# Two encoder layers on one core: the second MLP product by seven block products instead of eight

## The chip, the cores and the metric

The kernel runs on one core of one Trainium2 chip. The metric is the device time of one execution in microseconds (us). TensorE (PE in the profile) multiplies matrices into PSUM, VectorE (DVE), ScalarE (ACT) and GpSimd (POOL) do the elementwise work, and the queue of SyncE (SP) issues most of the loads from HBM.

## What is computed

The program is two layers of an encoder over 512 tokens of 1024 channels, in fp32. Each layer has four attention branches (A to D) that are gated, merged and projected, a LayerNorm, an MLP with a gated per-layer input, and a second LayerNorm. The lines that matter here are those of the MLP:

```python
h = layer_norm(alpha * h + merged @ w_out[i], ln1_g[i], ln1_b[i])
ff = jnp.square(jax.nn.relu(h @ w_ff1[i])) @ w_ff2[i]
ple = (p[i] @ w_ple[i]) * jax.nn.sigmoid(h @ w_ple_gate[i])
h = layer_norm(alpha * h + ff + ple, ln2_g[i], ln2_b[i])
```

`w_ff1` is 1024 by 4096 and `w_ff2` is 4096 by 1024.

## The kernel before

**Arithmetic.** PE reads operands of type fp32r. A factor x is held as two such tiles: hi, the rounded copy of x, and lo, which is x - hi. A product of two factors takes three matmuls, hi by hi, lo by hi and hi by lo (the list `SEQ3`). The tile `R` has 64 slots of 128x512 for hi and lo parts; 16 of them hold the residual stream h, and 48 are given out by an allocator (`P.ar`).

**Weights.** All weights come in chunks of 128x1024 (512 KB), in one list that `plan_layer` writes in the order of use. SP loads a chunk into one of two raw buffers; ACT copies it to its hi slots (line 106, called in `split_next`), and POOL subtracts to make its lo slots (line 170). `take` is called where PE's work on a chunk is written; it first writes out loads and splits up to some chunks ahead (`look`, `extra`), as far as slots are free.

**Order.** Nothing is scheduled: each engine runs its instructions in the order in which the program writes them, each waiting for what it needs. So an instruction that waits holds back everything behind it on its engine.

**MLP before.** Per layer there are 32 chunks of `w_ff1`. For each, PE makes 24 matmuls of 512 columns into one bank (`gemm_T`, line 94), ACT takes the relu out of PSUM (line 1291), DVE squares it (1293), ACT makes hi (106) and DVE makes lo (109). The 32 hidden tiles are taken in groups of 12, 12 and 8. After each group, `outer` multiplies them with the group's chunks of `w_ff2`: for either half f of the 1024 output columns, each chunk (two hidden tiles by 512 columns) takes 24 matmuls of 512 columns, six into each of four banks, one bank for 128 tokens. At the end of a half DVE adds the four banks to the residual rows `FD` (1303, 1305). The second product thus takes 32 chunks of 24 matmuls, 768 a layer.

**Branch B.** The last projection tile of stage A makes B's keys. `evac_k2` writes hi of either head into one half of the partitions of its slot and copies it into the other half by DVE (lines 365 and 366). The first score matmuls of branch B stand at the start of the next `run`, which deals out the steps of an attention branch evenly between the parts of the main work.

## Time and profile before

| | |
|---|---|
| time, median of 3 runs | 1996.1 us (1995.84 to 1997.12) |
| the profiled execution, its time | 1997.37 us |
| the profiled execution, its span | 1995.5 us |
| TensorE busy | 1954.3 us (98%), 9440 matmuls |
| VectorE busy | 777.1 us (39%) |
| ScalarE busy | 755.2 us (38%) |
| GpSimd busy | 840.3 us (42%) |
| granted TensorE clock, mean | 0.997 |

The span is the time from the first to the last instruction of the profiled execution; the 1.9 us beside it lie around the program. Busy time is that in which an engine works on at least one instruction. The profile says of each idle stretch of an engine which other instruction ended it; for one that isn't on the path that ends last, such idle time costs nothing.

### The profile page before, as it was taken

The page shows a single profiled execution, that of the slowest core. Times are in us where ns is not written, and L with a number is a line of the kernel's source. Part 1 is how long each engine was busy: PE and PEld are TensorE (multiplying, and loading weights), DVE is VectorE, ACT ScalarE, POOL GpSimd, SP SyncE. Part 2 cuts the span into 40 slices and gives each one's busy share as a digit, 9 for nine tenths or more (in the row PEclk, how much of TensorE's full clock was granted, in tenths as well). Part 3 has the DMA queues.
Part 4 walks back from the last instruction along what each step waited for, and adds up shares of the span by engine and source line. Part 5 has one row for each costly group of instructions (what it writes and reads, how often), then busy time and mean ns, then how long its engine had stood idle before and what let it go on. Part 6 is the DMA issues. An engine that isn't in the chain of part 4 may idle for free.

```text
span 1995.5 us, 24072 instructions
## 1 busy us (share of the span) xinstructions
PE 1954.3 (98%) x9440; PEld 1611.4 (81%) x9440; DVE 777.1 (39%) x1565; ACT 755.2 (38%) x1313; POOL 840.3 (42%) x407
## 2 busy tenths in 40 slices
...
GB/s 168 108 54 82 99 112 97 89 82 61 147 117 95 96 126 74 107 87 103 122 111 68 57 82 103 82 125 72 101 56 168 96 102 101 102 84 127 67 120 78
DMA packets 59697, 195.96 MB, mean 98 GB/s; under 512 B 6720, under 2 KB 11968, under 8 KB 59584
## 3 DMA queue, kind: packets, MB, share of 16 engines
...
## 4 chain that ended last, share of the span: by engine, by line
PE 66%; DVE 3%; ACT 1%; POOL 1%; DMA 1%; issue 1%; DVEq 0%; ACTq 0%; POOLq 0%
PE PS L94 64%; PE PS L97 2%; ACT R L106 1%; POOL R L170 1%; DVE R L109 1%; DMA raw<-in_wO_dram 0%; DMA raw<-in_wPL_dram 0%; DVE gate L1254 0%; DVE FD L303 0%; DVE FD L301 0%; DVE p L394 0%; ACT p L386 0%; DVE qf L916 0%; DVE ysum L421 0%; DVE rt L915 0%
## 5 line engine op out<-in xcount | busy, mean ns | idle before, releaser
L94 PE MATMUL PS<-R 128*128 128x512 f32 (+4 forms) x8528 | 1886.2, 378 | 12.3 <-DVE R L365 5.3
L94 PEld LDWEIGHTS PS<-R 128*128 128x128 f32 (+1 forms) x8528 | 1508.5, 187 | 333.0 <-issue 37.6
L170 POOL TENSOR_TENSOR R<-raw,R 128x1024 fp32r<-128x1024 f32 (+1 forms) x304 | 734.7, 2421 | 848.5 <-ACT R L106 811.2
L106 ACT ACTIVATE R<-raw 128x1024 fp32r<-128x1024 f32 x306 | 321.1, 1053 | 340.8 <-PE PS L94 143.5
L106 ACT ACTIVATE R<-PS 128x128 fp32r<-128x128 f32 (+5 forms) x300 | 131.7, 450 | 131.9 <-PE PS L97 82.3
L109 DVE TENSOR_TENSOR R<-PS,R 128x512 fp32r<-128x512 f32 (+5 forms) x276 | 134.4, 494 | 118.7 <-ACT R L106 117.5
L1109 POOL TENSOR_TENSOR M<-M,gate 128x512 f32<-128x512 f32 x48 | 62.1, 1293 | 191.7 <-DVE gate L1108 135.5
L386 ACT ACTIVATE p<-p,s 128x256 f32<-128x256 f32 (+2 forms) x96 | 66.1, 688 | 187.1 <-DVE s L551 65.4
L1293 DVE TENSOR_TENSOR ff<-relu 128x512 f32<-128x512 f32 x64 | 44.3, 692 | 222.1 <-ACT relu L1291 222.1
L1305 DVE TENSOR_TENSOR FD<-FD,PS 128x512 f32<-128x512 f32 x40 | 27.5, 687 | 242.5 <-PE PS L94 242.5
L1291 ACT ACTIVATE relu<-PS 128x512 f32<-128x512 f32 x64 | 38.3, 599 | 168.5 <-PE PS L94 168.5
L394 DVE TENSOR_SCALAR p<-p,s 128x512 f32<-128x512 f32 (+3 forms) x128 | 95.0, 742 | 4.5
L97 PE MATMUL PS<-ident,p 128*128 128x128 f32 x480 | 73.6, 273 | 2.8 <-DVE p L394 1.7
L97 PEld LDWEIGHTS PS<-ident,p 128*128 128x128 f32 x480 | 58.6, 140 | 16.1 <-DVE p L394 2.5
L109 DVE TENSOR_TENSOR R<-ff,R 128x512 fp32r<-128x512 f32 x64 | 44.3, 692 | 47.6 <-ACT R L106 47.6
L1108 DVE SCALAR_TENSOR_TENSOR gate<-gate,PS 128x512 f32<-128x512 f32 x48 | 32.9, 686 | 71.1 <-ACT gate L1104 42.8
L106 ACT ACTIVATE R<-ff 128x512 fp32r<-128x512 f32 x64 | 40.5, 632 | 50.9 <-DVE ff L1293 50.9
L393 DVE RECIPROCAL s<-s 128x1 f32<-128x1 f32 x128 | 20.9, 163 | 79.3 <-ACT p L386 78.1
L277 POOL TENSOR_TENSOR s<-s,mhalf 128x1 f32<-128x1 f32 x18 | 21.4, 1192 | 71.9 <-DVE s L275 71.9
L627 DVE CUSTOM_DVE_ANT_0 p<-PS,bd 128x512 f32<-128x512 f32 x32 | 21.8, 682 | 76.1 <-PE PS L94 76.1
L386 ACT ACTIVATE p<-PS,s 128x512 f32<-128x512 f32 x32 | 22.0, 689 | 53.2 <-DVE s L481 53.0
L106 ACT ACTIVATE R<-M 128x512 fp32r<-128x512 f32 (+3 forms) x20 | 13.8, 695 | 62.3 <-POOL M L1109 52.7
...
## 6 DMA issues: line engine op xcount, KB each, us to landing
raw<-in_wF_dram SPq DMA_DIRECT2D x128, 512.0 KB, 3.4
raw<-in_wT_dram SPq DMA_DIRECT2D x106, 512.0 KB, 3.5
raw<-in_wBR_dram SPq DMA_DIRECT2D x16, 512.0 KB, 3.5
raw<-in_wO_dram SPq DMA_DIRECT2D x16, 512.0 KB, 3.6
raw<-in_wPG_dram SPq DMA_DIRECT2D x16, 512.0 KB, 3.4
raw<-in_wVD_dram SPq DMA_DIRECT2D x12, 512.0 KB, 3.4
hsp<-FD SPq DMA_DIRECT2D x8, 512.0 KB, 6.1
FD<-hsp SPq DMA_DIRECT2D x8, 512.0 KB, 5.9
```

The lines of the kernel that those rows point to most:

```text
L94: self.nc.tensor.matmul(out, l, r, start=start, stop=stop, skip_group_check=True)
L97: self.nc.tensor.transpose(out, in_, self.ident)
L106: self.nc.scalar.activation(out=out, in_=in_, func=AF.Copy, scale=scale)
L109: self.nc.vector.tensor_tensor(out=out, in0=a, in1=hi.bitcast(F32), op=ALU.subtract)
L170: nc.gpsimd.tensor_tensor(out=lo, in0=raw, in1=hi.bitcast(F32), op=ALU.subtract)
L386: P.nc.scalar.activation(out=pt[:, 0:n], in_=src, func=AF.Exp, bias=nm, scale=1.0, accum_out=den)
L394: nc.vector.tensor_scalar(out=pt[:, 0:n], in0=pt[:, 0:n], scalar1=rd, scalar2=0.5, op0=ALU.mult, op1=ALU.mult)
L1108: nc.vector.scalar_tensor_tensor(out=t, in0=t, scalar=1.0, in1=pb, op0=ALU.add, op1=ALU.mult)
L1109: nc.gpsimd.tensor_tensor(out=P.M[:, j, :], in0=P.M[:, j, :], in1=t, op=ALU.add)
L1291: nc.scalar.activation(out=r, in_=ps, func=AF.Relu)
L1293: nc.vector.tensor_tensor(out=f, in0=r, in1=r, op=ALU.mult)
L1305: nc.vector.tensor_tensor(out=u, in0=u, in1=ps, op=ALU.add)
```

## The change

The second product of the MLP is made by Strassen's scheme in Winograd's form. Two hidden tiles (a pair) and 512 tokens make a left matrix of 2 by 2 blocks (hidden tile by half of the tokens), the two chunks of `w_ff2` that belong to the pair make a right one (hidden tile by half of the output columns). Seven products of blocks take the place of eight. The left factors are the blocks 11, 12 and 22 and four sums of blocks (`hidden`); the right factors are the blocks 11, 21 and 22 and four differences T1 to T4, which DVE makes in place in the raw buffers (`split_quad`). Each product takes 6 matmuls of 512 columns, three into each of two banks. There are 16 pairs a layer, in groups of 2, 3, 3, 3, 3 and 2; within a group each of the seven products runs over the group's pairs before the next begins. The first pair of the next group is made before a group's products.

Three pairs of banks (X, Y, Z) gather the products; X is read by DVE after P1, goes on with P6, is read again, and goes on with P7.

Raw buffers, the softmax tiles and some other tiles become parts of one tile `F`, so that in the MLP seven raw buffers can be had instead of two, and up to four chunks are loaded ahead. In `evac_k2` four ACT copies replace two ACT copies and two DVE copies; branch B's steps begin two parts later.

The tile `F` is what the orders below call the raw buffers, `ff` are squared hidden tiles, `fs` the sums of left blocks, `PS` PSUM, and `FD` the residual rows.

The core of the diff:

```diff
+U_P, U_PG, U_YS, U_RAW, N_UNIT = 16, 25, 29, 31, 39
...
-        self.raw_p = pool("raw", 2)
...
-        self.p_p = pool("pp", 3)
...
+        self.F = const.tile([128, N_UNIT, 256], F32, name="F")
+        self.M = self.F[:, 0:16, :].rearrange("p (a b) c -> p a (b c)", b=2)
+        self.pt = [self.units(U_P + 3 * i, 3) for i in range(3)]
+        self.pi = 0
+        self.ysum = self.units(U_YS, 2)
+        self.pg = self.units(U_PG, 4).rearrange("p (c t) -> p c t", c=4)
+        self.fa = Arena(N_UNIT)
+        self.fa.close(0, U_RAW)
...
-            self.load(self.cs + 2)
+            self.load(self.cs + self.depth)
...
+    def split_quad(self, c, only_make=False):
+
+
+        nc = self.nc
+        *q, what = c['quad']
+        (r0, u0), (r1, u1) = [self.raws.get(tuple(q) + (f,), (None, None)) for f in range(2)]
+        at = {'11': (r0, 0), '21': (r0, 512), '12': (r1, 0), '22': (r1, 512)}
+        b = lambda n: at[n][0][:, at[n][1]:at[n][1] + 512]
+        op = {'T1': ('11', '12', '11'), 'T2': ('11', '22', '11'), 'T3': ('12', '22', '12'), 'T4': ('21', '11', '21')}
+        src = what
+        if what in op:
+            src, x, y = op[what]
+            if not c.get('made'):
+                nc.vector.tensor_tensor(out=b(src), in0=b(x), in1=b(y), op=ALU.subtract)
+                c['made'] = True
+        if only_make:
+            return
+        c['k'] = 1
+        c['s'] = [self.ar.alloc(1) for _ in range(2)]
+        c['hi'], c['lo'] = [self.R[:, s, :] for s in c['s']]
+        self.acopy(c['hi'], b(src))
+        nc.gpsimd.tensor_tensor(out=c['lo'], in0=b(src), in1=c['hi'].bitcast(F32), op=ALU.subtract)
+        if what == 'T3':
+            self.fa.release(u1, 4)
+        elif what == 'T4':
+            self.fa.release(u0, 4)
...
+            self.split_quad(c)
+            self.cs += 1
+            if self.cs < self.cd and self.chunks[self.cs]['quad']:
+                self.split_quad(self.chunks[self.cs], True)
+            return
...
+    def run(self, main, other=(), after=0):
...
-                want = len(other) * seen // n_m
+                want = len(other) * max(seen - after, 0) // (n_m - after)
...
-    P.acopy(v(ka)[0:64], ps[0:64])
-    P.acopy(v(kb)[64:128], ps[64:128])
+    for x in (slice(0, 64), slice(64, 128)):
+        P.acopy(v(ka)[x], ps[0:64])
+        P.acopy(v(kb)[x], ps[64:128])
     P.vsub(v(kl)[0:64], ps[0:64], v(ka)[0:64])
     P.vsub(v(kl)[64:128], ps[64:128], v(kb)[64:128])
-    nc.vector.tensor_copy(ka[64:128], ka[0:64].bitcast(F32))
-    nc.vector.tensor_copy(kb[0:64], kb[64:128].bitcast(F32))
...
-FF_GROUPS = ((0, 12), (12, 24), (24, 32))
+
+FF_GROUPS = (2, 3, 3, 3, 3, 2)
+
+FF_LOOK = {'1': (2, 2, 9, 9), '2': (6, 1, 2, 0)}
+PRODUCTS = (('P1', '11'), ('P5', 'T1'), ('P6', 'T2'), ('P2', '21'), ('P3', '22'), ('P7', 'T3'), ('P4', 'T4'))
...
+def ff_order():
+
+    out, a = [], 0
+    for n in FF_GROUPS:
+        out += [('1', i) for i in range(a + bool(a), a + n)]
+        if a + n < 16:
+            out.append(('1', a + n))
+        out.append(('2', range(a, a + n)))
+        a += n
+    return out
...
+    for what, i in ff_order():
+        if what == '1':
+            for j in (2 * i, 2 * i + 1):
+                P.plan((l, 'f1', j), a['wF1'][l, j], 1024)
+            continue
+        for prod, right in PRODUCTS:
+            for q in i:
+                f = {'P1': 0, 'P5': 1}.get(prod)
+                P.plan((l, 'f2', prod, q), None if f is None else a['wF2'][l, f, q], 1024, quad=(l, q, right), half=f)
...
-    P.run(main, stB + pre(lambda: biasC(0)))
+    P.run(main, stB + pre(lambda: biasC(0)), 2)
...
-    for gi, (j0, j1) in enumerate(FF_GROUPS):
-        fs = []
-        for j in range(j0, j1):
-            w = P.take((l, 'f1', j))
-            ps = P.PS[:, P.bank(), :]
+
+    P.fa.close(0, 8, False)
+    P.fa.close(U_P, U_RAW - U_P, False)
+    P.depth, P.more = 4, 16
+    P.look, P.extra, P.reserve, P.least = FF_LOOK['1']
+    left = {}
+
+    def hidden(i):
+
+        f = P.bias_p.tile([128, 1024], F32, tag="bias", name="ff").rearrange("p (x t) -> p x t", x=2)
+        for x in range(2):
+            w = P.take((l, 'f1', 2 * i + x))
+            ps = P.PS[:, 5 + x, :]
             for _ in P.gemm_T(ps, w, 8, P.h_xs()):
                 pass
             P.done(w)
             r = P.tmp("relu")
             nc.scalar.activation(out=r, in_=ps, func=AF.Relu)
-            f = P.tmp("ff")
-            nc.vector.tensor_tensor(out=f, in0=r, in1=r, op=ALU.mult)
-            s = P.ar.alloc(1), P.ar.alloc(1)
-            fs.append(s)
-            P.split(P.R[:, s[0], :], P.R[:, s[1], :], f)
-        if gi == len(FF_GROUPS) - 1:
-            P.extra, P.more = 2, 9
-        for f in range(2):
-            def end(c, ps, f=f):
-                u = rows(P)[:, c, 512 * f:512 * f + 512]
-                if gi == 0 and f == 1:
+            nc.vector.tensor_tensor(out=f[:, x, :], in0=r, in1=r, op=ALU.mult)
+        s = [P.ar.alloc(n) for n in (1, 1, 2, 2, 1)]
+        R2 = lambda k: P.slot(s[k], 1).rearrange("p a (b t) -> p (a b) t", b=2)
+        P.split(R2(0), R2(1), f[:, :, 0:256])
+        S = P.bias_p.tile([128, 1024], F32, tag="bias", name="fs").rearrange("p (x t) -> p x t", x=4)
+        a11, a12, a21, a22 = f[:, 0, 0:256], f[:, 1, 0:256], f[:, 0, 256:512], f[:, 1, 256:512]
+        tt = nc.vector.tensor_tensor
+        tt(out=S[:, 0], in0=a21, in1=a22, op=ALU.add)
+        tt(out=S[:, 1], in0=S[:, 0], in1=a11, op=ALU.subtract)
+        tt(out=S[:, 2], in0=a11, in1=a21, op=ALU.subtract)
+        tt(out=S[:, 3], in0=a12, in1=S[:, 1], op=ALU.subtract)
+        S4 = lambda k: P.slot(s[k], 2).rearrange("p a (b t) -> p (a b) t", b=2)
+        P.split(S4(2), S4(3), S)
+        P.split(R2(4)[:, 0], R2(4)[:, 1], a22)
+        d = {'s': s}
+        for k, p in ((0, 'P1'), (1, 'P2')):
+            d[p] = R2(0)[:, k], R2(1)[:, k]
+        for k, p in enumerate(('P5', 'P6', 'P7', 'P3')):
+            d[p] = S4(2)[:, k], S4(3)[:, k]
+        d['P4'] = R2(4)[:, 0], R2(4)[:, 1]
+        left[i] = d
...
+    banks = {'X': (0, 1), 'Y': (2, 3), 'Z': (4, 7)}
+    where = {'P1': 'X', 'P6': 'X', 'P7': 'X', 'P5': 'Y', 'P3': 'Y', 'P2': 'Z', 'P4': 'Z'}
+    lo, hi, both = slice(0, 512), slice(512, 1024), slice(0, 1024)
+
+    gets = {'P1': (0, lo), 'P5': (1, hi), 'P6': (0, hi), 'P2': (0, lo), 'P3': (0, hi), 'P7': (1, both), 'P4': (1, lo)}
+
+    def second(pairs):
+        first = pairs[0] == 0
+        for prod, _ in PRODUCTS:
+            if prod == 'P6' and pairs[-1] == 15:
+                P.fa.close(0, U_RAW)
+            bs = banks[where[prod]]
+            fresh = prod in ('P1', 'P5', 'P2', 'P4')
+            for q in pairs:
+                w = P.take((l, 'f2', prod, q))
+                ww = w['hi'], w['lo']
+                for t in range(2):
+                    for n, (li, wi) in enumerate(SEQ3):
+                        P.mm(P.PS[:, bs[t], :], left[q][prod][li][:, 128 * t:128 * t + 128], ww[wi],
+                             fresh and q == pairs[0] and n == 0, q == pairs[-1] and n == 2)
+                P.done(w)
+                s = left[q]['s']
+                for k, n in {'P2': ((0, 1), (1, 1)), 'P7': ((2, 2), (3, 2)), 'P4': ((4, 1),)}.get(prod, ()):
+                    P.ar.release(s[k], n)
+            half, x = gets[prod]
+            for t in range(2):
+                ps = P.PS[:, bs[t], :]
+                u = rows(P)[:, 2 * half + t, x]
+                if prod == 'P7':
+                    u = u.rearrange("p (x t) -> p x t", x=2)
+                    ps = bass.AP(ps.tensor, ps.offset, [list(ps.ap[0]), [0, 2], [1, 512]])
+                if first and prod in ('P5', 'P6'):
                     nc.vector.scalar_tensor_tensor(out=u, in0=u, scalar=ALPHA, in1=ps, op0=ALU.mult, op1=ALU.add)
                 else:
-                    nc.vector.tensor_tensor(out=u, in0=u, in1=ps, op=ALU.add)
-            outer([(l, 'f2', f, i) for i in range(j0 // 2, j1 // 2)],
-                  lambda c, li, k: P.R[:, fs[k][li], 128 * c:128 * c + 128], end)
-        for s in fs:
-            P.ar.release(s[0], 1)
-            P.ar.release(s[1], 1)
+                    nc.vector.tensor_tensor(out=u, in0=u, in1=ps, op=ALU.subtract if prod == 'P4' else ALU.add)
+
+    for what, i in ff_order():
+        if what == '1':
+            hidden(i)
+            continue
+        P.look, P.extra, P.reserve, P.least = FF_LOOK['2']
+        second(i)
+        P.look, P.extra, P.reserve, P.least = FF_LOOK['1']
+    P.depth, P.more, P.least, P.reserve = 2, 9, 0, 4```

Two places show how the order moves. First DVE, where a group of hidden tiles ends and its second product begins; before:

```order
L1293 TENSOR_TENSOR ff<-relu 128x512
L109 TENSOR_TENSOR R<-ff,R 128x512
L1305 TENSOR_TENSOR FD<-FD,PS 128x512 x4
L1303 SCALAR_TENSOR_TENSOR FD<-FD,PS 128x512 x4
L1293 TENSOR_TENSOR ff<-relu 128x512
```

and with the change, at a group of three pairs:

```order
L1386 TENSOR_TENSOR ff<-relu 128x512
L133 TENSOR_TENSOR R<-ff,R 128x512
L1393 TENSOR_TENSOR fs<-ff 128x256
L1394 TENSOR_TENSOR fs<-fs,ff 128x256
L1395 TENSOR_TENSOR fs<-ff 128x256
L1396 TENSOR_TENSOR fs<-ff,fs 128x256
L133 TENSOR_TENSOR R<-fs,R 128x1024
L133 TENSOR_TENSOR R<-ff,R 128x256
L198 TENSOR_TENSOR F<-F 128x512 x2
L1442 TENSOR_TENSOR FD<-FD,PS 128x512 x4
L198 TENSOR_TENSOR F<-F 128x512 x2
L1442 TENSOR_TENSOR FD<-FD,PS 128x512 x2
```

Between the square of the last hidden tile and the first reading of a bank (L1442) there now stand the making of the left factors and two right differences (L198); further differences stand between the later readings.

Second ACT, around the first chunks of hidden tiles that follow a group's second product; before, within a group:

```order
L106 ACTIVATE R<-ff 128x512
L106 ACTIVATE R<-raw 128x1024 x13
L1291 ACTIVATE relu<-PS 128x512
L106 ACTIVATE R<-ff 128x512
L106 ACTIVATE R<-raw 128x1024
```

and with the change, from the last left factor before a group's products on:

```order
L130 ACTIVATE R<-ff 128x256
L130 ACTIVATE R<-F 128x512 x15
L130 ACTIVATE R<-F 128x1024 x6
L130 ACTIVATE R<-F 128x512 x3
L1385 ACTIVATE relu<-PS 128x512
L130 ACTIVATE R<-F 128x512 x2
L1385 ACTIVATE relu<-PS 128x512
L130 ACTIVATE R<-ff 128x512
```

The 15 copies are hi parts of right factors of the running group, the 6 are the next six chunks of `w_ff1`, the 3 are P1's right factors of the next group and the 2 its first two T1; these two stand ahead of the relu of the second hidden tile. POOL makes the lo parts in the same order.

## Rows read from the trace of the kernel before

**Rows 1.** The page: busy time by engine, and the chain that ended last.

```profile
PE 1954.3 (98%) x9440; PEld 1611.4 (81%) x9440; DVE 777.1 (39%) x1565; ACT 755.2 (38%) x1313; POOL 840.3 (42%) x407
PE 66%; DVE 3%; ACT 1%; POOL 1%; DMA 1%; issue 1%; DVEq 0%; ACTq 0%; POOLq 0%
```

**Rows 2.** Windows view: length, busy us (instructions) of PE, PEld, DVE, ACT, POOL, clock, DMA.

```profile
620.00:990.00 370.00, 370.00 (x1634) 306.39 (x1633) 70.97 (x105) 111.45 (x138) 167.38 (x73) 1.00 0.31 101
1620.00:1990.00 370.00, 366.31 (x1617) 302.98 (x1615) 81.33 (x125) 106.20 (x132) 158.75 (x71) 1.00 0.29 97
```

**Rows 3.** The chain of waits in time, layer 0: start, length, what.

```profile
609.66 386.27 PE PS L94 x1704
```

**Rows 4.** Who waited for whom, PE: total us, times, longest us.

```profile
PE PS L94 <- DVE R L365: 5.3, 2, 2.7
```

**Rows 5.** Timeline at the start of branch B: start, length, engine, instruction.

```profile
154.85 2.35 DVE L365 CAST R<-R 64x512 fp32r<-64x512 f32 x1
157.23 0.42 DVE L366 CAST R<-R 64x512 fp32r<-64x512 f32 x1
157.34 3.10 PE L94 MATMUL PS<-R 128*128 128x256 f32 x8 [2.69 <-DVE R L365]
```

**Rows 6.** Timeline of ACT, then DVE, at one hidden tile.

```profile
767.48 0.60 ACT L1291 ACTIVATE relu<-PS 128x512 f32<-128x512 f32 x1 [4.38 <-PE PS L94]
768.89 0.63 ACT L106 ACTIVATE R<-ff 128x512 fp32r<-128x512 f32 x1 [0.82 <-DVE ff L1293]
769.43 1.04 ACT L106 ACTIVATE R<-raw 128x1024 fp32r<-128x1024 f32 x1
...
768.11 0.69 DVE L1293 TENSOR_TENSOR ff<-relu 128x512 f32<-128x512 f32 x1 [5.38 <-ACT relu L1291]
769.56 0.69 DVE L109 TENSOR_TENSOR R<-ff,R 128x512 fp32r<-128x512 f32 x1 [0.76 <-ACT R L106]
```

**Rows 7.** Groups by line and form: count, busy us, mean ns, idle before.

```profile
L170 POOL TENSOR_TENSOR R<-raw,R 128x1024 fp32r<-128x1024 f32 x301 | 728.6, 2425 | 846.3 <-ACT R L106 809.1 <-issue 17.4 <-PE PS L94 15.8
L1109 POOL TENSOR_TENSOR M<-M,gate 128x512 f32<-128x512 f32 x48 | 62.1, 1293 | 191.7 <-DVE gate L1108 135.5 <-DVE s L393 47.8 <-PE PS L94 8.4
L1305 DVE TENSOR_TENSOR FD<-FD,PS 128x512 f32<-128x512 f32 x40 | 27.5, 687 | 242.5 <-PE PS L94 242.5
L109 DVE TENSOR_TENSOR R<-PS,R 128x256 fp32r<-128x256 f32 x64 | 26.8, 421 | 32.0 <-ACT R L106 31.7
L106 ACT ACTIVATE R<-raw 128x1024 fp32r<-128x1024 f32 x303 | 318.3, 1055 | 336.0 <-PE PS L94 143.5 <-DMA raw<-in_wF_dram 94.0 <-DMA raw<-in_wPG_dram 24.7
L106 ACT ACTIVATE R<-PS 128x256 fp32r<-128x256 f32 x64 | 24.2, 380 | 26.7 <-PE PS L97 18.7 <-DVE R L109 4.9 <-PE PS L94 2.9
```

**Rows 8.** Timeline of POOL, then DVE, around 293 us.

```profile
291.68 1.29 POOL L1109 TENSOR_TENSOR M<-M,gate 128x512 f32<-128x512 f32 x1 [3.29 <-DVE s L393]
292.93 2.52 POOL L170 TENSOR_TENSOR R<-raw,R 128x1024 fp32r<-128x1024 f32 x1
...
293.12 0.41 DVE L109 TENSOR_TENSOR R<-PS,R 128x256 fp32r<-128x256 f32 x1
295.00 1.00 DVE L109 TENSOR_TENSOR R<-ysum,R 128x512 fp32r<-128x512 f32 x1 [0.76 <-ACT R L106]
```

**Rows 9.** Timeline of POOL, then DVE, at the end of layer 0's attention half.

```profile
599.54 6.62 POOL L170 TENSOR_TENSOR R<-raw,R 128x1024 fp32r<-128x1024 f32 x2
...
599.27 1.28 DVE L303 SCALAR_TENSOR_TENSOR FD<-FD,s,gb 128x1024 f32<-128x1024 f32 x1
600.47 1.28 DVE L109 TENSOR_TENSOR R<-PS,R 128x512 fp32r<-128x512 f32 x2
601.67 2.24 DVE L301 SCALAR_TENSOR_TENSOR FD<-FD,s,gb 128x1024 f32<-128x1024 f32 x1
604.01 3.24 DVE L303 SCALAR_TENSOR_TENSOR FD<-FD,s,gb 128x1024 f32<-128x1024 f32 x1
```

**Rows 10.** DMA issues: count, KB each, median us to landing.

```profile
raw<-in_wF_dram SPq DMA_DIRECT2D x128, 512.0 KB, 3.4
```

71 lines of the change are left out of this document (44 added, 27 removed).

## The prediction, made before the run

> **What bounds the kernel now.** I read the page first. PE is busy for 98% of the span and holds two thirds of the chain that ended last; no other engine is busy for half of it [rows 1]. The windows view of the two MLPs shows PE busy all the time, at full clock, in layer 0, and all but 3.7 us of 370 in layer 1 [rows 2]. The chain of waits has a stretch from before layer 0's MLP to its end that is nothing but matmuls: 1704 in 386.27 us, 0.2267 us each [rows 3]. So what is saved on PE there is saved in full, and whatever makes PE wait is paid in full. Six matmuls, called a product step below, take 1.36 us; a hidden tile takes 24, 5.44 us. The waits of PE name one stall that the change touches, 5.3 us on a DVE copy [rows 4].
>
> **Matmuls.** A pair of hidden tiles takes 42 matmuls instead of 48, so 16 pairs save 96 a layer: 96 x 0.2267 = 21.8 us, 43.5 for both. The Trainium skill (TensorE: Matmul & The Clock Gate, Back-to-back issue gap) gives 131 ns for a sustained matmul of this length and 216 for an isolated one, by which 192 matmuls would be worth 25 or 41 us. The row's 0.2267 stands here: it is this kernel's own operands.
>
> **Branch B.** PE's first score matmuls wait 2.69 us for the copy of the keys, which took 2.35 us beside a POOL instruction [rows 5]; in both layers 5.3 us [rows 4]. The copies go to ACT, and two parts (16 matmuls) come first. I take all 5.3 off. At worst ACT is late by half of that (2.7); that B's later steps then stand closer costs nothing that I can see, as their number is the same.
>
> **What the elementwise engines get.** Per pair, POOL had four splits of 1024 columns, 2.4 us each [rows 7]. Now it has two of those and seven of 512, at 1.29 each, 1.25 apart when they follow each other [rows 7, 8]. DVE gets four differences, four sums of 256 columns and wider splits. PE needs 90 x 0.2267 = 20.4 us a pair, POOL 13.6. That would hide, but two things stand against it.
>
> The first is that POOL and DVE exclude each other. A DVE instruction with both inputs in SBUF, 0.69 us otherwise [rows 6], began at 295.00 while POOL worked until 295.45 and ended at 296.00, 0.55 after POOL; one that reads PSUM took its usual 0.41 in the same stretch [rows 8]. Two POOL splits with two such DVE instructions in their way took 6.62 us instead of 4.85, and DVE got its turn between them [rows 9, 7]. So they take turns. A difference T (two SBUF inputs) costs POOL 0.55 us; the readings of a bank, with one, cost none.
>
> The second is order. In a group's product phase let t = 0 be the start of the last hidden tile's relu, which is nearly when PE begins P1. At one hidden tile the lo part is done 2.77 us after relu began [rows 6]. Behind it on DVE now stand the sums (1.4 to their end, at 0.42 each and partly dependent [rows 7]), ACT's copy of them (1.05 [rows 7]), its lo part (1.28, from a DVE instruction of that width [rows 9]), a short split (0.3), two T, and only then the reading of bank X after P1; DVE starts such instructions 0.6 apart (two in 1.28 [rows 9]). So 2.8 + 1.4 + 1.1 + 1.3 + 0.3 + 1.2 + 0.7 gives t = 8.7, or 9.8 if POOL's next split slips between (1.13 of port time: 1.29 less the 0.16 that its start takes). P6 goes on in bank X, so PE waits for that reading. Its due time is 36 matmuls, 8.2, in a group of three and 24, 5.4, in a group of two.
>
> - **Groups of two.** 9.8 or 8.7 against 5.4: 3.2 to 4.4; I take 3.7 for the first and 4.5 for the last, where relu comes late behind T copies. Together 8.2 a layer.
> - **Product phases of the four groups of three.** The reading costs 0.5 to 1.6; I take 1.6, as POOL has work there. Then right factors: nine at most are ahead, and the eighth needs a T that DVE made just before the reading. It is ready at 10.5. From there to the fifteenth POOL has seven splits and five turns of DVE: 7 x 1.25 + 5 x 0.55 = 11.5, so t = 22.0; PE wants it at 9.8 + 8 x 1.36 + 0.45 (lo comes third) = 21.1. About 1.0 late. Together 2.6 each, 10.4 a layer; bounds 0.5 and 3.3.
> - **The hidden tiles after them.** PE ends the 21 steps at about 31. POOL ends the last factor at 22.0 + 6 x 1.25 = 29.5, then has six `w_ff1` splits, 14.4, and P1's first lo part: 45.2. T1 overwrites that raw block, so DVE and then ACT wait for it, and for a second one; both ACT copies stand ahead of the second tile's relu, which so ends at 49.2 to 51. The fourth tile needs that bank, at 31 + 3 x 5.44 = 47.4. About 2.2 lost; then the third tile's relu stands behind the first pair's left factors: 0.8 more. Three a layer (the first such stretch follows a short phase, where POOL is done early): 9.0; bounds 1.2 and 5.5 each.
>
> Loads cost nothing: the same 512 KB pieces, 3.4 us each [rows 10], issued as POOL frees raw buffers; the P1 chunks land about 5 us before POOL reaches them. Without that cover a wait would fall into the third term. The extra readings of banks (DVE, 0.69 us each) lie beside matmuls of other banks. POOL's small LayerNorm instructions queue behind the next layer's splits, as now.
>
> **Sum.** Per layer 8.2 + 10.4 + 9.0 - 21.8 = +5.8; both layers +11.6; branch B -5.3: +6.3. Against the profiled execution, 1997.4, that is 2003.7; the median of the runs shown is 1.3 lower, so **2002 us**. The low bounds of all terms (6.4, 2.0, 3.6) give about 1971, the high ones (9.5, 13.2, 16.5, B at 2.7) about 2028.
>
> **Rivals.**
> - **Faster: POOL's lead holds after the phases.** If splits of `w_ff1` come early enough that no relu is held, the third term goes: -11.7, **1984**. For it: POOL is idle for more than half of the span [rows 1]. Against: it idles for want of slots before, not after, the product phase. It decides from 3 us of lead on.
> - **Faster: the turns cost next to nothing.** Then a phase of three loses 0.7 and a stretch 1.2: 8 + 2.8 + 3.6 - 21.8 = -7.4 a layer, -20 in all, **1976**. Against: rows 8 and 9.
> - **All of it hidden:** -43.5 - 5.3, **1947**. Against: the reading of bank X in the groups of two, which no lead helps.
> - **Slower: the pair of engines is the bound.** Per group of three POOL holds 6 x 2.4 + 21 x 1.25 = 40.7 and DVE's two-input work 19.2 (per pair seven at 0.55, five of half size at 0.28, one at 1.14), 59.9 against PE's 61.2. If gaps leave 15% unused, a group takes 70 instead of 65.3 now (288 x 0.2267); 5.3 groups and two layers: +50, less 5, **2040**. The Trainium skill (SBUF — State Buffer, Who interferes with whom) states the rule behind it: one lock, held for the whole instruction, the other engine blocked. By that rule the two sums add, and rows 8 and 9 agree.
>
> That fewer matmuls are not made at all is no rival: each product stands as six.
>
> **How the numbers follow.** A measurement of this kernel tells 0.2%, 4 us, from no change. Forecast 0.50, its own range 1993 to 2014, of which 0.11 lies within 4 us; lead holds 0.17; turns cheap 0.18; all hidden 0.06; bound by the pair 0.09. Faster: 0.15 + 0.18 + 0.06 = 0.39; same: 0.11 + 0.02 = 0.13; slower: 0.39 + 0.09 = 0.48. The range leaves out the last two cases and the lower edge of the third: 1971 to 2014.
>
> **What would show it.** Right: 9248 matmuls; PE waits for L1442 (bank X) some 4 us, twice a layer, and some 1 to 2 us four times; PE waits for POOL lo parts in the middle of product phases and for relu (L1385) after them; DVE's T at up to 1.8 us where POOL is busy; no wait for the keys. Wrong: an MLP without PE idle (then 1947 to 1976), T at 0.69 throughout (turns), or relu never waited for (lead). PE idle all through the product phases, with POOL and DVE without gaps, would be the last rival.

## The result, and the profile after

The changed kernel takes **2064.97 us** (median of 4 runs, 2063.59 to 2068.11), the kernel before 1995.97 beside it: ratio 1.0347, 95% interval 1.0329 to 1.0365. It is slower by 69 us, where 6 were forecast, and outside the range (1971 to 2014). The profiled execution took 2063.9 us and has a span of 2062.1 us against 1995.5.

The page after, busy time by engine and the chain that ended last (before: [rows 1]):

```profile
PE 1945.8 (94%) x9248; PEld 1590.5 (77%) x9248; DVE 1100.4 (53%) x1953; ACT 852.6 (41%) x1525; POOL 1007.2 (49%) x567
PE 36%; DVE 6%; ACT 3%; issue 2%; POOL 2%; DMA 1%; DVEq 0%; ACTq 0%; POOLq 0%
```

The 192 matmuls are gone. Yet PE is busy for 1945.8 us, where the 1954.3 of before less the forecast 43.5 would be 1910.8: the matmuls that are left take 35.0 us longer. The rest of the span, in which PE stands, is 116.3 us instead of 41.2, or 75.1 more. With the 43.5 saved, these two make the 66.6 us between the spans.

The shares in the second line are of the whole span, and the chain was not found all the way back: it adds up to 50% of the span here and to 73% before. Of the part that was found PE held nine tenths before (66 of 73) and holds seven tenths now (36 of 50); the rest went to DVE, ACT and POOL. (The forecast read the 66% as two thirds of the chain.)

Who PE waited for (total us, times, longest; the stall of [rows 4] is gone):

```profile
PE PS L118 <- ACT R L130: 27.8, 14, 5.7
PE PS L121 <- DVE FD L372: 20.8, 3, 11.0
PE PS L118 <- ACT relu L1385: 19.5, 11, 3.5
PE PS L118 <- DVE FD L1442: 18.2, 4, 7.3
PE PS L121 <- DVE F L462: 6.8, 4, 2.6
PE PS L118 <- ACT vd L130: 4.7, 2, 2.4
```

Each of these has a place. The first row holds eight stalls of 1.9 us ahead of P6, one in each group of three, and two of 5.7 and 5.3 in the last groups of two. At these P6 PE waits for two engines, and the profile names the one whose last instruction ended later, a copy on ACT. It is bank X that they wait for: PE begins 0.15 us after DVE's reading of that bank in all eight, and in the run lo_on_dve below it begins just as far behind the reading while the ACT copy that is named has not ended.

**The first group of two.** The timeline around 670 us, of POOL, DVE, then PE:

```profile
662.95 6.34 POOL L206 TENSOR_TENSOR R<-F,R 128x512 fp32r<-128x512 f32 x4 [5.53 <-ACT R L130]
...
664.66 3.48 DVE L1386 TENSOR_TENSOR ff<-relu 128x512 f32<-128x512 f32 x2
...
673.34 1.42 POOL L206 TENSOR_TENSOR R<-F,R 128x512 fp32r<-128x512 f32 x1 [4.06 <-issue]
673.56 1.48 DVE L133 TENSOR_TENSOR R<-ff,R 128x256 fp32r<-128x256 f32 x1
...
676.17 1.27 DVE L1442 TENSOR_TENSOR FD<-FD,PS 128x512 f32<-128x512 f32 x2
...
676.90 7.37 PE L118 MATMUL PS<-R 128*128 128x512 f32 x21 [7.28 <-DVE FD L1442]
```

Two squares take 3.48 us instead of 1.4, because four POOL splits run beside them and each square gets a turn only between two of them; the last short split of the left factors takes 1.48 instead of 0.42. The last relu began at 664.81 and the first reading of bank X ends some 0.69 after 676.17, at t = 12.1 (the forecast's 8.7 to 9.8 was for that end), and PE stands 7.28 us.

**A group of three.** The timeline of one period, of POOL alone, then of DVE, ACT and PE at its end:

```profile
735.22 20.36 POOL L206 TENSOR_TENSOR R<-F,R 128x512 fp32r<-128x512 f32 x14 [1.63 <-ACT R L130]
755.53 14.24 POOL L237 TENSOR_TENSOR R<-F,R 128x1024 fp32r<-128x1024 f32 x6
769.72 5.90 POOL L206 TENSOR_TENSOR R<-F,R 128x512 fp32r<-128x512 f32 x4
...
805.12 20.45 POOL L206 TENSOR_TENSOR R<-F,R 128x512 fp32r<-128x512 f32 x14 [1.62 <-ACT R L130]
```

```profile
771.05 1.75 DVE L198 TENSOR_TENSOR F<-F 128x512 f32<-128x512 f32 x1 [12.23 <-POOL R L206]
...
774.43 2.35 DVE L198 TENSOR_TENSOR F<-F 128x512 f32<-128x512 f32 x2
776.21 0.63 ACT L130 ACTIVATE R<-F 128x512 fp32r<-128x512 f32 x1 [2.74 <-DVE F L198]
776.74 0.58 ACT L1385 ACTIVATE relu<-PS 128x512 f32<-128x512 f32 x1
...
777.38 1.22 PE L118 MATMUL PS<-R 128*128 128x512 f32 x2 [2.83 <-ACT relu L1385]
...
795.70 0.60 ACT L1385 ACTIVATE relu<-PS 128x512 f32<-128x512 f32 x1 [4.32 <-PE PS L118]
```

From the second T2 factor on POOL works 40.4 us without a pause: the group's lo parts, six `w_ff1` chunks, the next P1 factors and the first T1. Behind each P1 factor DVE can make the T1 that overwrites the block POOL was reading, with a turn of POOL's in between; ACT copies it, and the relu of the second hidden tile, behind that copy, lets PE go on. The forecast had that relu end at t = 49.2 to 51; it ends at 51.5 (777.32, the last relu before the group having begun at 725.85). Three more tiles on PE end with the relu at 795.70, and 9.4 us behind that POOL has the next group's second T2 (805.12): a circle of 69.9 us.

The windows view from one P6 to the next, the first and the fifth of six such periods, and the sum of all six (length, then busy us of PE, PEld, DVE, ACT, POOL; in the rows, the matmuls in brackets and the granted clock behind POOL):

```profile
735.83:805.73 69.90, 65.11 (x271) 52.80 (x271) 42.91 (x54) 27.66 (x43) 44.50 (x28) 0.95 0.25 91
1828.93:1898.02 69.09, 63.30 (x270) 50.13 (x271) 41.74 (x54) 27.54 (x43) 44.60 (x28) 1.00 0.25 92
sum 418.21, PE 386.62 PEld 309.83 DVE 254.50 ACT 165.63 POOL 267.41; mean PE 64.44 PEld 51.64 DVE 42.42 ACT 27.61 POOL 44.57
```

A period takes 69.7 us on average. In it PE stands for 5.3 us and is busy for 64.4, where 270 matmuls of 0.2267 us are 61.2. POOL and DVE are each busy for under two thirds of it.

**The clock.** The windows view: length, busy us (instructions) of PE, PEld, DVE, ACT and POOL, granted clock, DMA.

```profile
665.00:669.00 4.00, 4.00 (x19) 3.31 (x18) 3.24 (x3) 1.03 (x2) 4.00 (x3) 1.00 0.00 0
677.00:680.00 3.00, 3.00 (x7) 2.41 (x8) 3.00 (x4) 0.63 (x1) 3.00 (x3) 0.50 0.00 0
682.00:684.00 2.00, 2.00 (x10) 1.61 (x9) 0.69 (x1) 1.48 (x2) 2.00 (x2) 1.00 0.76 252
```

After the 7.28 us stall PE runs at 0.50, the 1.2 GHz level: 7 matmuls in 3 us, 0.43 each, then again 10 in 2. Such stretches, 3.4 to 10.2 us long, begin in or behind 17 of the 28 waits of over 0.9 us from 140 us on. Within the span the granted clock is at half for 86.6 us, 10.9 before. The trace of the kernel before has one behind the stall of [rows 5]:

```profile
158.00:162.00 4.00, 4.00 (x12) 3.13 (x12) 1.32 (x6) 1.45 (x5) 0.00 (x0) 0.57 0.53 173
```

**The layer boundary.** The timeline of ACT, then of PE, at the end of layer 0:

```profile
1013.09 1.01 ACT L130 ACTIVATE R<-F 128x960 fp32r<-128x960 f32 x1 [9.64 <-DMA F<-in_wCQ_dram]
1014.51 1.01 ACT L130 ACTIVATE R<-F 128x960 fp32r<-128x960 f32 x1 [0.42 <-DMA F<-in_wCQ_dram]
1019.42 0.74 ACT L130 ACTIVATE R<-F 128x640 fp32r<-128x640 f32 x1 [3.90 <-DMA F<-in_wCQ_dram]
1021.92 1.06 ACT L130 ACTIVATE R<-F 128x1024 fp32r<-128x1024 f32 x1 [1.76 <-DMA F<-in_wKV_dram]
1024.95 1.06 ACT L130 ACTIVATE R<-F 128x1024 fp32r<-128x1024 f32 x1 [1.97 <-DMA F<-in_wKV_dram]
1025.92 0.58 ACT L1338 ACTIVATE gate<-PS 128x512 f32<-128x512 f32 x1
```

```profile
1037.51 1.97 PE L121 MATMUL PS<-ident,FD 128*128 128x128 f32 x8 [11.01 <-DVE FD L372]
```

Five copies of the next layer's weights stand on ACT ahead of the first gate and wait for their loads; the LayerNorm behind that gate holds PE for 11.0 us (before: 2.2 in two stalls).

### The profile page after: what moved, and what is told of

It is laid out like the page before. It is cut to its first block, busy times and chain, and to the rows that moved or that the text cites. A ratio compares the mean times of both kernels' runs of the same rounds, so it can differ in the third digit from the quotient of the medians.

```text
span 2062.1 us, 24818 instructions
## 1 busy us (share of the span) xinstructions
PE 1945.8 (94%) x9248; PEld 1590.5 (77%) x9248; DVE 1100.4 (53%) x1953; ACT 852.6 (41%) x1525; POOL 1007.2 (49%) x567
## 4 chain that ended last, share of the span: by engine, by line
PE 36%; DVE 6%; ACT 3%; issue 2%; POOL 2%; DMA 1%; DVEq 0%; ACTq 0%; POOLq 0%
PE PS L118 34%; ACT R L130 2%; PE PS L121 2%; DMA F<-in_wF_dram 1%; DVE F L198 1%; POOL R L206 1%; DVE R L133 1%; DVE ff L1386 1%; POOL R L237 0%; DVE FD L1442 0%; ACT relu L1385 0%; DVE F L462 0%; ACT F L454 0%; DVE qf L1003 0%; DVE fs L1393 0%
## 5 line engine op out<-in xcount | busy, mean ns | idle before, releaser
L118 PE MATMUL PS<-R 128*128 128x512 f32 (+5 forms) x8336 | 1877.9, 382 | 75.7 <-ACT R L130 27.8
L118 PEld LDWEIGHTS PS<-R 128*128 128x128 f32 (+2 forms) x8336 | 1486.7, 190 | 410.2 <-ACT R L130 34.1
L237 POOL TENSOR_TENSOR R<-F,R 128x1024 fp32r<-128x1024 f32 (+1 forms) x243 | 584.3, 2418 | 495.6 <-ACT R L130 446.9
L130 ACT ACTIVATE R<-F 128x1024 fp32r<-128x1024 f32 (+2 forms) x502 | 407.2, 835 | 441.8 <-DVE F L198 142.1
L206 POOL TENSOR_TENSOR R<-F,R 128x512 fp32r<-128x512 f32 x224 | 325.3, 1483 | 267.7 <-ACT R L130 244.9
L133 DVE TENSOR_TENSOR R<-PS,R 128x512 fp32r<-128x512 f32 (+5 forms) x276 | 134.7, 494 | 135.4 <-ACT R L130 132.0
L130 ACT ACTIVATE R<-PS 128x128 fp32r<-128x128 f32 (+4 forms) x320 | 143.9, 459 | 150.1 <-PE PS L121 97.5
L198 DVE TENSOR_TENSOR F<-F 128x512 f32<-128x512 f32 x128 | 145.3, 1168 | 110.9 <-POOL R L206 98.4
L1196 POOL TENSOR_TENSOR F<-F,gate 128x512 f32<-128x512 f32 x48 | 62.1, 1293 | 191.6 <-DVE gate L1195 139.4
L1442 DVE TENSOR_TENSOR FD<-FD,PS 128x512 f32<-128x512 f32 (+1 forms) x160 | 116.5, 761 | 54.3 <-PE PS L118 54.2
L462 DVE TENSOR_SCALAR F<-F,s 128x512 f32<-128x512 f32 (+3 forms) x128 | 100.8, 788 | 4.5
L1386 DVE TENSOR_TENSOR ff<-relu 128x512 f32<-128x512 f32 x64 | 74.5, 1168 | 53.3 <-ACT relu L1385 53.2
L121 PE MATMUL PS<-ident,F 128*128 128x128 f32 x504 | 79.0, 274 | 9.1 <-DVE F L462 6.8
L121 PEld LDWEIGHTS PS<-ident,F 128*128 128x128 f32 x504 | 61.5, 140 | 23.5 <-DVE F L462 8.1
L1385 ACT ACTIVATE relu<-PS 128x512 f32<-128x512 f32 x64 | 37.4, 588 | 70.4 <-PE PS L118 70.4
L133 DVE TENSOR_TENSOR R<-ff,R 128x512 fp32r<-128x512 f32 x64 | 54.0, 844 | 23.3 <-ACT R L130 23.3
L130 ACT ACTIVATE R<-fs 128x1024 fp32r<-128x1024 f32 x32 | 33.9, 1060 | 75.6 <-DVE fs L1396 75.6
L133 DVE TENSOR_TENSOR R<-fs,R 128x1024 fp32r<-128x1024 f32 x32 | 39.2, 1225 | 37.3 <-ACT R L130 37.3
## 6 DMA issues: line engine op xcount, KB each, us to landing
F<-in_wF_dram SPq DMA_DIRECT2D x128, 512.0 KB, 5.3
F<-in_wT_dram SPq DMA_DIRECT2D x106, 512.0 KB, 3.5
F<-in_wBR_dram SPq DMA_DIRECT2D x16, 512.0 KB, 3.5
F<-in_wO_dram SPq DMA_DIRECT2D x16, 512.0 KB, 3.5
F<-in_wPG_dram SPq DMA_DIRECT2D x16, 512.0 KB, 3.6
F<-in_wVD_dram SPq DMA_DIRECT2D x12, 512.0 KB, 3.4
hsp<-FD SPq DMA_DIRECT2D x8, 512.0 KB, 5.2
FD<-hsp SPq DMA_DIRECT2D x8, 512.0 KB, 6.0
```

Of the source, the lines that this page charges most:

```text
L118: self.nc.tensor.matmul(out, l, r, start=start, stop=stop, skip_group_check=True)
L121: self.nc.tensor.transpose(out, in_, self.ident)
L130: self.nc.scalar.activation(out=out, in_=in_, func=AF.Copy, scale=scale)
L133: self.nc.vector.tensor_tensor(out=out, in0=a, in1=hi.bitcast(F32), op=ALU.subtract)
L198: nc.vector.tensor_tensor(out=b(src), in0=b(x), in1=b(y), op=ALU.subtract)
L206: nc.gpsimd.tensor_tensor(out=c['lo'], in0=b(src), in1=c['hi'].bitcast(F32), op=ALU.subtract)
```

## The experiments

Times are single runs where no interval is given, each with the kernel before on the same chip (1995.9 to 1998.7). The runs p2_before_p6, mix and best1 to best7 also set the allocator of `R` back to its first slot behind the MLP (`P.ar.at = 0`), which their diffs below leave out. Two groups of three, from the end of one relu wait to that of the second next, show as one window. The changed kernel and four of the runs below, in the order changed kernel, fill, p2_before_p6, small_loads, relu_first:

```profile
777.38:917.66 140.28, 129.75 (x541) 104.16 (x541) 84.72 (x107) 55.31 (x84) 89.20 (x55) 0.96 0.26 90
```

```profile
774.97:915.62 140.65, 131.62 (x557) 104.40 (x557) 83.49 (x107) 55.16 (x84) 89.29 (x55) 0.98 0.25 90
```

```profile
772.96:912.89 139.93, 131.47 (x541) 101.61 (x541) 88.31 (x107) 55.56 (x84) 92.44 (x55) 0.98 0.25 91
```

```profile
776.71:916.85 140.14, 130.50 (x541) 105.21 (x541) 85.21 (x107) 54.50 (x84) 88.97 (x55) 0.95 0.04 12
```

```profile
784.43:916.23 131.80, 125.22 (x540) 102.20 (x540) 88.97 (x107) 54.90 (x85) 91.01 (x54) 0.99 0.27 96
```

### What a wait costs PE: stalls

```diff
+            m = {2: 1, 4: 2, 6: 3, 8: 4, 10: 5}.get(j % 12, 0) if j < 24 else 0
+            if m:
+                t = P.tmp("wait")
+                for _ in range(m):
+                    nc.vector.tensor_copy(t, ps)
             nc.scalar.activation(out=r, in_=ps, func=AF.Relu)
+            if m:
+                P.mm(ps, P.R[:, P.hh, 0:128], P.R[:, P.hh + 1, :], True, True)
```

> The kernel before, in which ten matmuls of each layer's MLP, far apart, must wait for one to five DVE copies out of PSUM (0.69 us each); nothing else of the change. The waits should be about 1.0, 1.7, 2.4, 3.1 and 3.8 us, two of each in a layer: 48 us in all, and 20 further matmuls 4.5 us. Theory (a stall of PE costs its length and then a stretch at half clock, 3.4 us of it after a stall of 1.9 in the changed kernel, of which half is lost): waits of 2.4 and more bring 1.7 us each besides, the shortest none, so 12 x 1.7 = 20 us more, about 2069 us, 2076 if the 1.7 us waits bring it too. Rival (the clock fell in the changed kernel for another reason, such as the busier DVE and POOL): clock 1.00 after each wait, 2049 us.

2088.71 us, 92.8 more than before. The relu read the bank after the copies, so the waits were longer than meant, 1.47 to 4.37 us, 58.4 in all (the trace's sum), and the 20 matmuls are 4.5; 29.9 us are left, near the theory's 20 to 27. The 49 matmuls after a wait of 1.47, 2.20, 2.92 and 3.65 us:

```profile
646.53:657.94 11.41, 11.41 (x49) 9.12 (x49) 2.75 (x4) 3.76 (x5) 4.67 (x2) 1.00 0.23 86
660.14:673.14 13.00, 12.99 (x49) 10.26 (x49) 2.74 (x4) 3.76 (x5) 4.66 (x2) 0.87 0.17 56
676.05:689.10 13.05, 13.05 (x49) 10.25 (x49) 2.75 (x4) 3.75 (x5) 4.64 (x2) 0.87 0.13 42
692.74:706.57 13.83, 13.82 (x49) 10.89 (x49) 2.75 (x4) 3.75 (x5) 4.65 (x2) 0.81 0.11 38
```

DVE, ACT and POOL do the same work in all four rows; after the longer waits the granted clock fell (means of 0.87 and 0.81) and the matmuls took 1.6 and 2.4 us more. None of the four waits of 1.47 us brought that, two of the four of 2.20, three of the four of 2.92, and all eight longer ones did. So where PE sets the pace, as in this kernel, a stall costs its length and the slow matmuls behind it, and the cause of these is the stall, not busier engines.

### Filling the stalls: fill

```diff
+            if prod == 'P6':
+                for _ in range(8 if len(pairs) == 3 else 30 if first else 8):
+                    P.mm(P.PS[:, 4, :], P.R[:, P.hh, 0:128], P.R[:, P.hh + 1, :], True, True)
```

> The changed kernel with matmuls that nobody reads, into a free bank, in front of each P6: 8 in groups of three (1.8 us, the length of the stall there), 30 in the first group of two, 8 in the last. Theory (the stall itself is set by DVE's chain, and the half clock after it by the stall): the clock stays at 1.00 there, and the time falls by what the half clock cost, 8 x 1.7 in the groups of three and 2 x 2.5 in the first groups of two: about 2046 us. Rival A (POOL and DVE together are the pace of the MLP, PE's stalls only show it): whatever PE gains at full clock it waits for elsewhere, 2060 to 2070 us. Rival B (the clock falls for another reason): clock still 0.5 after P6 begins, 2065 us or more.

2064.41 us. The stalls at P6 and the half clock after them went (clock 0.985 over the span, 0.979 before the edit), and nothing was gained: two groups take 140.65 us instead of 140.28. This is what rival A said. The half clock after P6 was no loss in these groups, since PE then waits for relu anyway.

### P2 ahead of P6: p2_before_p6

```diff
-PRODUCTS = (('P1', '11'), ('P5', 'T1'), ('P6', 'T2'), ('P2', '21'), ('P3', '22'), ...
+PRODUCTS = (('P1', '11'), ('P5', 'T1'), ('P2', '21'), ('P6', 'T2'), ('P3', '22'), ...
```

> The changed kernel with the products in the order P1, P5, P2, P6, P3, P7, P4, so that bank X is wanted again 18 matmuls (4.1 us) later in a group of three, 12 (2.7 us) in one of two. Theory (the reading of bank X comes late by a fixed time, since DVE's chain after the last hidden tile has a fixed length): the eight stalls of 1.9 us go with their half clock (1.7 each), those of 7.3 us become about 4.6: 29 + 5 = 34 us, about 2031 us. Rival A (POOL and DVE are the pace): the time comes back as later waits, for POOL's lo parts in the product phase and for relu after it: 2055 to 2065 us.

2053.75 us. The first groups gained (3.8 us of stall instead of 7.3). In the groups of three the stalls at P6 went, and again a group kept 70 us: small steps of PE for lo parts took their place, in which two matmuls begin 0.3 to 0.55 us apart instead of 0.23.

### Lo parts on DVE: lo_on_dve and mix

```diff
-        nc.gpsimd.tensor_tensor(out=c['lo'], in0=b(src), in1=c['hi'].bitcast(F32), op=ALU.subtract)
+        self.vsub(c['lo'], b(src), c['hi'])
```

> The changed kernel with the lo parts of all right factors made by DVE instead of POOL: POOL loses 224 instructions of 1.25 us, DVE gets 224 of 0.69 us. Theory (POOL's lag after a product phase and the turns between POOL and DVE hold the relu and with it PE): the waits for relu go (19.5 us, and the half clock after the longer of them), and DVE's squares and left factors take 0.69 us again; the bank X reading stays about where it is, one or two more 0.69 us instructions ahead of it and no POOL turn. About 2035 us, 2015 to 2050. Rival (it is the number of instructions in DVE's own order that makes PE wait, not POOL): DVE gets 155 us more work in the MLPs and PE waits longer at P6: 2080 us or more.

2054.51 us. Both were half right. The relu waits went, and a group takes 68.0 us (135.92 for two). PE stands 4.8 to 5.0 us at P6 instead, in eight groups. The profile names ACT's copies of right factors, but PE begins 0.15 us after the reading of bank X, as in the changed kernel, and on DVE that reading now stands behind lo parts:

```profile
PE PS L118 <- ACT R L130: 45.4, 14, 5.0
```

Two of the seven lo parts on DVE, with P2 ahead of P6 and the edit of the run boundary (below):

> The changed kernel with three edits: P2 ahead of P6, no splits beyond the gate chunks in the last group, and the lo parts of the right blocks 21 and 22 (two of seven) made by DVE. Theory (pace of the pair of engines): of a group of three POOL loses 6 x 1.25 us and DVE gains 6 x 0.69, so that the sum in which they exclude each other falls by 3.4 and the group from 70 to 66.5 us: 2053.8 - 10 - 3.4 x 5.3 x 2 = about 2008 us. Rival (DVE's own order: what stands ahead of the reading of a bank and of T decides): groups stay at 68 or more, as with all lo parts on DVE, 2030 to 2045 us.

2055.74 us, and 68.2 us a group: PE waits 4.3 us in each. With this order of the products the wait is not at P6 but at P7, which goes on in bank X and needs the reading after P6. On DVE that reading (744.47) stands behind three differences, the last T3 and two T4, two of which take a turn behind POOL; the timeline of DVE, then PE:

```profile
740.26 4.29 DVE L198 TENSOR_TENSOR F<-F 128x512 f32<-128x512 f32 x3
744.47 1.27 DVE L1445 TENSOR_TENSOR FD<-FD,PS 128x512 f32<-128x512 f32 x2
...
745.29 1.19 PE L118 MATMUL PS<-R 128*128 128x512 f32 x2 [4.33 <-ACT R L130]
```

It is the rival's mechanism, what stands ahead of a reading on DVE, at more than its price. The edit of the run boundary also adds waits of 5.2 and 4.7 us at the ends of the two layers (below).

### Are the loads on the loop? small_loads

```diff
-            self.nc.sync.dma_start(out=c['raw'][:, 0:c['n']], in_=c['src'])
+            if c['key'][1] in ('f1', 'f2') and self.cd >= 4:
+                self.nc.sync.dma_start(out=c['raw'][:, 0:128], in_=c['src'][:, 0:128])
+            else:
+                self.nc.sync.dma_start(out=c['raw'][:, 0:c['n']], in_=c['src'])
```

> The changed kernel, but of every chunk of w_ff1 and w_ff2 only the first 128 of 1024 columns are loaded, so that the two MLP products use partly old numbers; every instruction and every wait is kept. Theory (the loop that makes a group of three last 70 us goes through the loads: the raw buffers of a group come free only with its last differences T3 and T4, the next chunks are loaded 5 to 9 us after that, and POOL's lo parts, T1 and relu stand behind them): loads land in some 2 us, ACT no longer waits for them (77.6 us in all before), the relu waits go, a group takes 64 to 67 us: 10 groups x 4, some 2020 to 2035 us. Rival (POOL and DVE in turns are slow enough by themselves): groups stay at 69 to 70 us, 2055 to 2066 us.

2066.38 us, 140.14 for two groups. The loads landed in 1.9 us instead of 5.3 (DMA view):

```profile
F<-in_wF_dram SPq DMA_DIRECT2D x128, 64.0 KB, 1.9
```

The chain of waits of the changed kernel runs through these loads (7.7, 9.1 and 8.8 us in three groups of layer 1). A chain names the one that came last of two: with the load away, POOL's own row of splits takes its place. The theory of the raw buffers fell here.

### Relu ahead of the splits: relu_first

```diff
+            P.extra = 0
             w = P.take((l, 'f1', 2 * i + x))
...
             nc.vector.tensor_tensor(out=f[:, x, :], in0=r, in1=r, op=ALU.mult)
+            P.extra = FF_LOOK['1'][1]
+            P.ahead(P.ci, P.ci + P.look, P.ci + P.more)
```

> The changed kernel, but in the stretches of hidden tiles the splits made ahead are written behind the relu and the square of each tile instead of in front of its matmuls. Theory of order (the relu waits are only copies of T that stand ahead of relu on ACT): the waits of 2.8 to 3.5 us go with their half clock, 6 x 3 + some 10, about 2038 us. Rival (a group of three takes 70 us because POOL and DVE, taking turns, can't make its factors in less; the runs with filled stalls and with P2 ahead of P6 both kept 70): PE waits for lo parts or bank X instead, still about 70 us a group, 2055 to 2068 us.

2044.23 us, and 131.80 for two groups, 65.9 each, with the same work on POOL (91.01 us busy against 89.20) and DVE. So the pair of engines does not need 70 us; the order in which the splits ahead are written made it 70. The edit moves two links of the circle: the second tile's relu ends 41.8 us behind the start of the last relu instead of 51.5, since it no longer stands behind copies of T1 on ACT, and POOL's row of lo parts ends at 26.8 instead of 29.7. What each is worth was not separated. Some of the gain was given back where the square of the first group is delayed further (a stall of 11.4 us) and at the boundary (14.2).

### Left factors later, and the boundary: defer, boundary, stop

```diff
...
+            if prod == 'P5' and held:
+                held()
...
```

> The changed kernel, but the left factors of the next group's first pair are written behind the readings of P5 instead of ahead of the products. Theory (DVE's and ACT's chain for these factors, 6.7 us from 668.2 to 675.0 in the changed kernel's first group, makes the reading of bank X late): the stalls at P6 go, 7.3 to under 1 in the first groups, with some 2.5 of half clock each, 1.9 to 0 in the groups of three. In these the gain may be taken back by relu waits, as it was with filled stalls. So 18 us from the first groups for certain, up to 15 + some clock from the others: 2030 to 2048 us. Rival (T's and POOL's turns make the reading late, not these factors): stalls at P6 stay over half as long, 2055 us or more.

2048.62 us, just over the upper end: the first group's stall fell from 7.28 to 2.53 us, the stalls at P6 in groups of three went, these groups took 68.1 us, and the boundary grew to 13.6.

```diff
+        if i[-1] == 15:
+            P.look, P.extra, P.more = 4, 0, 4
```

> The changed kernel, but in the last group of products no chunks beyond the four gate chunks are split ahead. Theory (the 11.0 us stall before the next layer's first transposes: on ACT five hi copies of the next layer's weights stand ahead of the first gate and wait for loads that the two raw buffers let go late): the gates come when PE is done with them, the stall falls to 2 or 3 us and most of the half clock behind it (10.2 us in the changed kernel) goes: 9 + 4, about 2052 us. Rival (the weights come late anyway, because POOL frees raw buffers late): the wait moves to the next layer's first projection, 2060 to 2066 us.

2072.33 us. The stalls at the boundary are 0.44 and 1.63 us, but the products of the last group starved (5.1 and 1.1 us): the cap held back their factors too. With a stop at the next layer's first chunk instead:

```diff
+            P.stop = 1 + max(n for n, c in enumerate(P.chunks) if c['key'][:2] == (l, 'pg'))
...
```

> The changed kernel, but while the last group of products is written no chunk of the next layer is split ahead (the run 'boundary' also cut the number of right factors ahead to four, which starved the products themselves by 6.6 us; here that number stays). Theory: the next layer's hi copies no longer stand ahead of the gates on ACT, the 11.0 us stall ahead of the next layer's transposes falls to about 2, as in 'boundary', and the half clock there mostly goes: 9 + 4, about 2052 us. Rival: the loads come late anyway and the wait moves into the next layer's first projections, 2060 to 2066 us.

2060.14 us: the stalls are 0.44 and 1.62 us at the boundary, and 2.52 later for a lo part of the next layer. The mechanism is the theory's; the time is the rival's, 4.8 us less where 13 were forecast, and part of the wait moved on.

### Branch B's part alone: b_alone

This is the kernel before with `evac_k2` and `run(..., 2)` of the change.

> The kernel before with branch B's part of the change alone: four ACT copies in evac_k2, branch B's steps two parts later; the MLP as before. By the prediction: the two stalls of 2.69 go and nothing comes for them, -5.3, about 1990.7 us. Theory from the changed kernel's trace: they go with their half clock, but a wait for vd grows from 1.02 to 2.37 and one of 2.55 for the softmax normalisation is new, in both layers, with half clock of their own: -5.3 - 3.4 + 7.8 and 0 to 7, so 1995 to 2002 us.

2000.49 us against 1997.7, ratio 1.0012 (1.0002 to 1.0021), 10 and 13 runs: no gain, and at most 0.2% of loss. The two new stalls of the changed kernel are here without its MLP:

```profile
182.04 2.82 PE L94 MATMUL PS<-R 128*128 128x512 f32 x14 [2.37 <-ACT vd L106]
...
213.83 0.55 PE L97 MATMUL PS<-ident,p 128*128 128x128 f32 x3 [2.55 <-DVE p L393]
```

### Together: best1, best2, best3, best5, best6, best7

> The changed kernel with four edits together: splits ahead behind relu, left factors of the next group's first pair behind P5's readings, no next-layer chunk split ahead in the last group, branch B's part as it was before the change. Theory (the loss is a sum of waits in the engines' orders, each with its own place, and the half clock behind them): from 2044 us, 2 x (10 + 5) in the first groups, 8 x 1.5 at bank X, 12 + 5 at the layer boundary, 3 in branch B: about 1982 us, faster than the kernel before. Rival (POOL with DVE sets a pace near the old one, 65 us a group): what is taken off comes back as waits for lo parts and relu, 2000 to 2015 us.

2040.47 us. Here relu waits of 3.9 to 4.3 us returned (68 us a group): the deferred factors stand ahead of T3 and T4 on DVE. The first groups still stall for 6.6 us.

> As best1, with P2 ahead of P6 besides, so that T2's factors and bank X are wanted 4 us later. If T2 (made by DVE, then copied by ACT) is what P6 waits for once the readings are early, this is faster than best1 by up to 10 us; if nothing waits at P6 any more it is the same within 3 us; if P3 and P7 then wait for their later T's it is slower.

2040.54 us, the same, with 3.9 to 4.1 us at P7 in place of the relu waits. As in mix, PE waits there for the reading of bank X after P6, behind T3 and T4 on DVE.

> The changed kernel with the splits ahead behind relu in all stretches but the one ahead of the first group, the left factors behind P5's readings in the first group alone, no next-layer chunk split ahead in the last group, and branch B's part as before the change. The run 'relu_first' had groups of 65 to 67 us, those with left factors deferred everywhere 68, since deferring them delays T3 and T4 and so the raw buffers. Theory (loop through the raw buffers): groups stay at 65 to 67 here, the first groups lose 2.5 instead of 11.4 (and 5 of half clock), the boundary 2 to 5 instead of 14.2: 2044 - 28 - 15 - 3 = 1998 us. Rival (a pace of 68 us): 2020 to 2035 us.

2015.35 us against 1998.68, between the theory's 1998 and the rival's 2020. Groups take 65.9 us, the first group stalls for 2.5 and 2.4, and the stalls at the boundary are 0.4 and 1.6 as before the change, with 2.5 later. It is the best form found, and still slower than the kernel before. PE's waits in it (L1454 is the reading of a bank):

```profile
PE PS L118 <- DVE FD L1454: 20.5, 12, 2.5
PE PS L118 <- ACT relu L1388: 11.8, 8, 2.0
PE PS L118 <- ACT R L130: 9.2, 6, 3.9
```

> As best3, with the products in the order P1, P5, P6, P3, P7, P2, P4 and P4 gathered in banks Y: T3, and with it the second raw buffer of each pair, comes one product (4 us) earlier. Theory (loop through the raw buffers): the next loads begin 4 us earlier for half of the buffers, and the relu waits of 1.8 us shrink: 2 to 4 us a group less than best3, about 1975 to 1990 us. Rival (the loop goes through T4 and the first buffers, or not through loads at all): within 5 us of best3.

2031.25 us, 16 slower than best3. This speaks against the raw buffers once more. The groups of three keep their length (66.2 us from P1 to P1 on average, 65.7 in best3); from the first group of two to the next it is 61.9 and 62.8 us in the two layers, where best3 takes 57.9.

> As best3, with groups of 3, 3, 3, 3, 3 and 1 pairs instead of 2, 3, 3, 3, 3 and 2, so that the last pair's hidden tiles are made ahead of a product phase like the others. Theory (separate waits, each with its own place): the last group's stalls (5.7 us a layer and 3.4 of half clock) become some 2 in the one short phase, the first group's 5.3 become about 2: 2 x (5 + 3) less than best3, about 1999 us. Rival (the short last group, 42 matmuls in 9.5 us, starves for T's and bank X): what is gained in the first group is lost there, 2010 to 2020 us.

2020.73 us, ratio 1.0114 (1.0099 to 1.0129): the first group's stall moved to a relu wait of 4.3 us and the short last group kept 5.3.

> As best6, with P2 ahead of P6. If the 1.53 us at P6 in every group of three are bank X's reading alone, they go, as in the run 'p2_before_p6': 8 to 10 x 1.5, some 12 to 15 us less than best6. If T2's copy comes no earlier than now, PE waits for that instead (4 us a group, as in the run 'mix'): 20 us more than best6.

2031.53 us, ratio 1.0167 (1.0150 to 1.0183). In the first group PE waits 5.0 us at P7, as in mix, for the reading of bank X behind T3 and T4 (the copy of T2, which the expectation went by, is not what it waits for), and later for relu (3.6 to 4.8).

## Why the prediction was wrong

The direction was the likelier of the two, and most mechanisms stood where they were put. The sum fell short by 63 us (2065 against 2002), or by 60 from the profiled executions (2063.9 against 2003.7).

**The step that failed most is the price of a wait**, in the words of the forecast "whatever makes PE wait is paid in full". The sum took a wait at its length and every matmul at 0.2267 us. Of the 60 us 35 are matmuls that took longer than that, for which it had no term: PE was busy for 60.6 us at half clock, 6.8 before, which is some 27 of the 35, and the rest is small steps. The other 25 are idle time: 50 us more than before were forecast (55 of waits less the 5 of branch B), 75 came. The run stalls shows that such waits alone slow the matmuls behind them, and the stall of [rows 5] already had it behind it.

By terms:

- **Matmuls, -43.5:** right, 9248 matmuls; the 0.2267 us held wherever the clock was full and nothing was waited for.
- **Groups of three: right parts, wrong sum.** Forecast were 2.6 us in the product phase and 3.0 at relu, 66.8 us a group; it took 69.7. PE's idle time was as forecast (5.3 us), and the 2.9 are its slower matmuls, 1.9 us a group by the clock. Seen as a circle, POOL's row of lo parts ended at t = 29.7 (forecast 29.5), the relu at 51.5, where the sum took 49.6 out of its own 49.2 to 51; 16.3 for three tiles and up to 1.7 of half clock follow. The half clock alone doesn't set the length: the period from 1828.93 had full clock throughout and took 69.1 us. "Paid in full" fails here the other way too, for PE doesn't set the pace: what it loses or gains between T2 and relu, as at P6, counts nothing (fill, p2_before_p6). Edits of the circle's links made it shorter: 65.9 us in relu_first, 68.1 in defer, 68.0 in lo_on_dve.
- **Groups of two: mis-sized.** Forecast were 8.2 us a layer; measured are 15.7 and 14.7, 14.0 more in all, and some 10 of half clock. The first has 7.3 at bank X where 3.7 were forecast. In the last, 5.7 and 5.3 go to the last pair's left factors, a wait that the forecast did not have, up to 0.9 to steps behind it, and 1.8 to bank X. The forecast let POOL delay the chain of the left factors by one split at most; squares and left factors wait for it too (1.74 us a square where POOL has a row of splits).
- **Turn-taking: right.** T and squares took 1168 ns on average where 690 were free, POOL's short split 1483 ns where 1250 and 550 for each turn of DVE were taken:

```profile
L206 POOL TENSOR_TENSOR R<-F,R 128x512 fp32r<-128x512 f32 x224 | 325.3, 1483 | 267.7 <-ACT R L130 244.9 <-PE PS L118 12.9 <-issue 9.9
L198 DVE TENSOR_TENSOR F<-F 128x512 f32<-128x512 f32 x128 | 145.3, 1168 | 110.9 <-POOL R L206 98.4 <-DMA F<-in_wF_dram 12.5
L1386 DVE TENSOR_TENSOR ff<-relu 128x512 f32<-128x512 f32 x64 | 74.5, 1168 | 53.3 <-ACT relu L1385 53.2
```

- **The boundary at nothing: wrong.** It took 8.8 us more than before, and a stretch of half clock. The text named POOL's queue; it was ACT's, and the loads ahead of it. The run stop took the 11.0 us off and found 2.5 of them again later.
- **Branch B, -5.3: wrong.** "That B's later steps then stand closer costs nothing" failed: 1.35 and 2.55 us of new waits came in each layer; measured alone it is 0.12% slower, some 2.4 us.
- **Loads at nothing: right within the MLP** (small_loads), though they took 5.3 us instead of 3.4 and the chain ran through them; at the boundary ACT's copies waited for them.
- **The rivals.** The pair of engines as the bound gave 70 us for a group, which is what came; but that is luck, for relu_first and best3 made it in 65.9 with the same work, so its reason was wrong. Lead and cheap turns did not occur.

Why the periods differ by up to 1.4 us (68.9 to 70.3), why best5's first groups are longer, and what keeps best3 17 us over the kernel before stay open; of best3's waits the list above has the places. best6's PE stands as long as best3's; its matmuls take 5.9 us longer.
